# The low part of a mixing weight made by ScalarE and an adding transfer, with other changes around the RMS norms

## The chip, the cores and the metric

The kernel runs on one core of one Trainium2 chip. The metric is the device time of one execution in microseconds (us). TensorE is called PE here, VectorE DVE, ScalarE ACT, GpSimd POOL, and SyncE SP; SP's queue starts nearly all transfers of the kernel before. "PEld" is the loading of a product's stationary operand, which runs beside the products.

## What is computed

One layer of a hybrid decoder, in float32, for a prompt of 1024 tokens and 64 sample tokens (8 sequences of 8). The reference, cut to what matters:

```python
x = x + 0.5 * swiglu(rmsnorm(x, g1), ffn1_w_in, ffn1_w_out)      # D_FF = 2816
proj = rmsnorm(x, gm) @ w_in                                     # 1024 x 8224: u, z, x/B/C, dt, gates
branch_pool = pool_mix(u) @ pool_w_out                           # windowed means, 4 groups
y = ssd_scan(conv(x/B/C), dt)                                    # Mamba-2, chunks of 128
yg = y * silu(z);  yg = yg * rsqrt(mean(yg * yg per group of 512) + eps)
branch_ssd = (yg * ssd_norm) @ ssd_w_out
x = x + (sigmoid(g0) * branch_pool + sigmoid(g1) * branch_ssd) @ w_o
x = x + 0.5 * swiglu(rmsnorm(x, g2), ffn2_w_in, ffn2_w_out)
y = rmsnorm(x, norm_final)
```

## The kernel before, in words

**Tiling and stages.** Activations lie feature-major: 128 features on the partitions, tokens along the row. The tokens are worked in two halves: half 0 has 512 prompt tokens, half 1 has the other 512 and the 64 sample tokens (576). There are three stages, each with its own pool of buffers that is opened when the pool of the stage before is closed: `ffn1`, `mix` and `ffn2`. The mixing stage goes through half 0 and then half 1 (`mix_half`). In a half, PE first computes dt, then the pooling branch with its gate (tiles u, G0, `pool_w_out`), then four SSD groups. For each group it projects six conv tiles (`proj_group`), runs the scan as a chain beside the next group's projections, then z, then `ssd_w_out` of the group before; last come the gates, the merge and `w_o`.

**Precision.** A float32 matrix product is made of three products in a faster 32-bit format (float32r): weight and activation are each split into a rounded part hi and a rest lo, and PE adds hi·hi, hi·lo and lo·hi (`products`). A chunk of weights is 128 x 512 numbers (four blocks of 128 rows, 256 KB). `load_w` loads the chunk into a buffer `wraw` (6 buffers), ACT copies it rounded into `wh` (L274, 3 buffers), and DVE subtracts that from the chunk and writes the rest into `wl` (L275, 3 buffers). A chunk feeds 12 products of 512 columns in half 0, and 24 of 288 in half 1. The mixing stage uses 396 chunks. The SwiGLU stages use `load_w` too, for their first three column tiles (`ffn_in_plain`) and for the outgoing product; their other chunks go through `wino_weights`, which the change leaves alone.

**The RMS norms.** `rstd` is called 12 times: once for each half ahead of the mixing stage and once for each half ahead of ffn2 (by `norm_split` and `norm_parts`), and eight times in the gating of the SSD groups (`gating`). It squares and adds the tiles on ACT and DVE, sums over the partitions with one-column products on PE (`pss`, L160), and has the mean of 128 tokens in each column of a small tile `rsm`. `newton` then computes 1/sqrt on DVE: 11 small instructions (L322 to L327). After that PE transposes `rsm` (`prt`), ACT copies it out of PSUM (`rt`, L362), a transfer writes it to DRAM (`rd`, L363), and another reads it back, repeated on all 128 partitions, into `r` (L365). The tiles are multiplied by `r` on DVE (L1264 in the gating) and split again into hi and lo (L312 on ACT, L314 or L316 on DVE). `newton` is also used at the start, on the input blocks (`load_x`, L652 to L659), and at the end, in the final norm (L1431 to L1440).

**The order of the work.** The program is written as one stream of products; small chains (norms, scan, gating) are generators that are stepped between the products by a clock that counts the PE time written so far. A `yield 3.0` means "go on 3 us of PE time later". `R_WAIT0` is the wait between the reciprocal root and its transposition, and `R_WAIT` the wait between the transfer that reads `r` and its first use. Each engine works its own list in order. The weight split is written under `high_priority(40)`, which puts it earlier in the lists of ACT and DVE than where it is written.

Of the kernel before, what the change touches and what calls it, by code (L numbers as in the profile page):

```python
# [8 lines left out]
F32 = mybir.dt.float32  # L9
F32R = mybir.dt.float32r  # L10
I32 = mybir.dt.int32
AF = mybir.ActivationFunctionType
ALU = mybir.AluOpType

P = 128
# [20 lines left out]
N_ACT, N_BIG, N_PD = 58, 3, 4  # L36
N_RAW, N_W = 6, 3
N_FX, N_S, N_PDF = 17, 4, 6
# [11 lines left out]
MP = 2.0  # L50
R_WAIT0 = 3.0
R_WAIT = 5.0
F_Y = 0.5
# [8 lines left out]
def tile_hybrid_pool_ssd_macaron(  # L62
# [19 lines left out]
    def nm(s):  # L82
        uid[0] += 1
        return f"{s}_{uid[0]}"
# [78 lines left out]
    def tr(out, in_, idn):  # L163
        T.transpose(out, in_, idn)  # L164
        pe[0] += 0.107
# [10 lines left out]
    G.memset(ones, 1.0)  # L176


    rows = []
# [40 lines left out]
    Dcol = cp.tile([P, 16], F32, tag="Dcol", name="Dcol")  # L220
    rd_n = [0]
    hp = [0]
# [33 lines left out]

    ahead = {}

# [4 lines left out]
    def load_w(w, k0, nk, c0, ncol=P, behind=None):  # L263

        if (k0, c0) in ahead:
            return ahead.pop((k0, c0))
        raw, wh, wl = (sp.tile([P, 4 * P], d, tag=t, bufs=n, name=nm(t))[:, : nk * ncol]
                       for t, d, n in (("wraw", F32, N_RAW), ("wh", F32R, N_W), ("wl", F32R, N_W)))
        if behind is not None:
            hold(raw, behind)  # L270
        dma(raw.rearrange("p (k c) -> p k c", c=ncol),
            w[k0 * P : (k0 + nk) * P, c0 : c0 + ncol].rearrange("(k p) c -> p k c", p=P))
        with tc.high_priority(hp[0]):
            S.activation(wh, raw, AF.Copy)  # L274
            V.tensor_tensor(wl, raw, wh.bitcast(F32), op=ALU.subtract)  # L275
        return wh.rearrange("p (k c) -> p k c", c=ncol), wl.rearrange("p (k c) -> p k c", c=ncol)
# [40 lines left out]

    def newton(ss, fr):


        r, t = fr
        V.tensor_scalar(r.bitcast(I32), ss.bitcast(I32), -0.5, 1597463007.0, op0=ALU.mult, op1=ALU.add)  # L322
        V.tensor_scalar_mul(ss, ss, -0.5)
        for _ in range(3):
            V.tensor_tensor(t, r, r, op=ALU.mult)
            V.tensor_tensor(t, t, ss, op=ALU.mult)
            V.scalar_tensor_tensor(r, t, 1.5, r, op0=ALU.add, op1=ALU.mult)  # L327

    def rstd(tiles, h, count, out, pace=1.0):
# [23 lines left out]
        if h == 1:  # L353
            V.tensor_scalar(sm[:NS, 2, 4:5], pt[:NS, 4:5], 1.0 / count, EPS, op0=ALU.mult, op1=ALU.add)
        newton(v, (sm[:, 0, :nch], sm[:, 1, :nch]))
        yield R_WAIT0
        rd = dp.tile([5, P], F32, tag=f"rd{rd_n[0] % 4}", name=nm("rd"))
        rd_n[0] += 1
        pt = psum("ps", "prt")
        tr(pt[:nch, :P], sm[:, 0, :nch], ident)  # L360
        rt = act((P, P), name="rt")
        S.copy(rt[:nch], pt[:nch, :P])  # L362
        dma(rd[:nch], rt[:nch])  # L363
        r = act((P, N), name="r")
        dma(r, rd.rearrange("c p -> (c p)")[:N].partition_broadcast(P))  # L365
        yield R_WAIT
# [259 lines left out]
    def load_x(h, out):  # L626
# [26 lines left out]
        V.tensor_scalar(v, v, 1.0 / D, EPS, op0=ALU.mult, op1=ALU.add)  # L653
        newton(v, (ss[:, 2, :nb], ss[:, 3, :nb]))
        yield 0.5
# [766 lines left out]
    def final(g):  # L1422
# [9 lines left out]
        V.tensor_scalar(ss[:, 0, :nb], ss[:, 0, :nb], 1.0 / D, EPS, op0=ALU.mult, op1=ALU.add)  # L1432
        newton(ss[:, 0, :nb], (ss[:, 2, :nb], ss[:, 3, :nb]))
        for i, (_, dst, c0, n) in enumerate(parts[g]):
# [74 lines left out]
```

## Time and profile before

| | |
|---|---|
| time, median of 3 runs | 2989.13 us (2988.89 to 2989.58) |
| profiled execution: time, and span of its instructions | 2992.09 us, 2990.3 us |
| PE busy, share of the span | 2911.7 us, 97% |
| PEld | 2688.9 us, 90% |
| DVE | 1745.6 us, 58% |
| ACT | 1268.3 us, 42% |
| POOL | 410.3 us, 14% |
| mean granted TensorE clock | 0.993 |

How to read it: all times in the views count from the first instruction of the profiled execution. Its own time is 1.8 us above its span, and 3.0 us above the median of the runs. In a view of groups, a row has the line, the engine, the operation, what is written and read, the number of instructions, then the busy time, the mean ns of one, and the engine's idle time just before them with what ended it. In a timeline a row has start, length, engine, line and operation, the number of instructions merged into it, and in brackets the idle time before it with its releaser. A busy PE row is a modelled length, since products overlap; what counts for its pace is the distance from start to start.

### The profile page before, as it was taken

How to read it: one execution, taken by the hardware profiler on the slowest of the kernel's cores; microseconds unless marked ns; L12 is line 12 of the kernel's file. 1: busy time of each engine (PE TensorE's matmuls, PEld its weight loads, DVE VectorE, ACT ScalarE, POOL GpSimd, SP SyncE). 2: the span in 40 equal slices, each digit the busy share in tenths (PEclk: the TensorE clock that was granted, in tenths of full speed). 3: DMA queues.
4: the chain of work that ended last, by engine and by line, in shares of the span. 5: the costliest groups of instructions: out<-in, count | busy, mean ns of one | idle time of the engine just before them, and what ended most of it. 6: DMA issues, size and time to landing. Idle time of an engine off the chain costs nothing. (4 is left out here: it accounts for less than half of the span.)

```text
span 2990.3 us, 51513 instructions
## 1 busy us (share of the span) xinstructions
PE 2911.7 (97%) x19668; PEld 2688.9 (90%) x19668; DVE 1745.6 (58%) x3460; ACT 1268.3 (42%) x2560; POOL 410.3 (14%) x501
## 2 busy tenths in 40 slices
PE   7999999999999999999999999999999999999998
PEld 6999999789988878877999989999989999997898
DVE  6544344445373897877725987978775343444442
ACT  5343334433243665434424655543443333343432
POOL 5333333000000000000000110100023333330000
PEclk9999999999999999999999999999999999999999
DMA  4443223654334433445333344254443222235552
GB/s 137 137 130 100 70 83 98 220 171 121 105 100 121 115 103 96 117 119 172 101 101 107 97 127 137 84 141 134 152 136 97 77 84 69 84 95 170 173 160 71
DMA packets 519275, 352.09 MB, mean 118 GB/s; under 512 B 27163, under 2 KB 460433, under 8 KB 519019
## 3 DMA queue, kind: packets, MB, share of 16 engines
q1 hardware_dynamic: 519010, 348.80, 38.9%
q8 instruction: 154, 2.52, 0.3%
q14 instruction: 95, 0.77, 0.1%
q10 hardware_dynamic: 16, 0.00, 0.0%
HBM read 291.65 MB, written 57.29 MB: 117 GB/s over the span
## 5 line engine op out<-in xcount | busy, mean ns | idle before, releaser
L274 ACT ACTIVATE wh<-wraw 128x512 fp32r<-128x512 f32 (+1 forms) x636 | 391.5, 618 | 811.5 <-PE po L160 250.8
L275 DVE TENSOR_TENSOR wl<-wraw,wh 128x512 fp32r<-128x512 f32 (+1 forms) x636 | 438.0, 690 | 480.1 <-ACT wh L274 458.3
L160 PE MATMUL pw<-hi,wh 128*128 128x288 f32 (+1 forms) x1216 | 352.3, 290 | 4.0 <-DVE t L526 2.2
L160 PE MATMUL pw<-hi,wl 128*128 128x288 f32 (+1 forms) x1216 | 351.5, 289 | 0.0
L160 PE MATMUL pw<-lo,wh 128*128 128x288 f32 (+1 forms) x1216 | 351.2, 289 | 0.0
L160 PE MATMUL pw<-X,wh 128*128 128x288 f32 (+1 forms) x1824 | 347.4, 289 | 0.1
L160 PE MATMUL po<-hh,wh 128*128 128x288 f32 (+1 forms) x1056 | 289.4, 330 | 7.5 <-ACT hh L312 6.3
L160 PE MATMUL po<-hr,wh 128*128 128x288 f32 (+1 forms) x1056 | 289.4, 329 | 0.5 <-DVE hr L314 0.5
L160 PE MATMUL po<-hh,wl 128*128 128x288 f32 (+1 forms) x1056 | 289.0, 328 | 0.0
L160 PEld LDWEIGHTS pw<-X,wh 128*128 128x128 f32 x1824 | 288.1, 190 | 0.4 <-ACT t L522 0.4
L160 PE MATMUL pw<-X,wl 128*128 128x288 f32 (+1 forms) x912 | 263.0, 288 | 0.0
L160 PEld LDWEIGHTS pw<-hi,wh 128*128 128x128 f32 x1216 | 230.8, 190 | 4.9 <-DVE t L526 2.6
L160 PEld LDWEIGHTS pw<-lo,wh 128*128 128x128 f32 x1216 | 230.8, 190 | 0.0
L160 PEld LDWEIGHTS pw<-hi,wl 128*128 128x128 f32 x1216 | 230.8, 190 | 0.0
L422 DVE TENSOR_TENSOR wl<-s,wh 128x512 fp32r<-128x512 f32 x160 | 114.1, 714 | 175.6 <-ACT wh L421 172.8
L160 PEld LDWEIGHTS po<-hh,wh 128*128 128x128 f32 x1056 | 179.2, 189 | 26.5 <-ACT hh L312 11.4
L160 PEld LDWEIGHTS po<-hr,wh 128*128 128x128 f32 x1056 | 179.9, 189 | 17.8 <-DVE hr L314 4.1
L160 PEld LDWEIGHTS po<-hh,wl 128*128 128x128 f32 x1056 | 180.0, 189 | 14.4 <-DVE wl L275 0.9
L421 ACT ACTIVATE wh<-s 128x512 fp32r<-128x512 f32 x160 | 101.0, 632 | 179.8 <-PE pw L160 178.7
L160 PEld LDWEIGHTS pw<-X,wl 128*128 128x128 f32 x912 | 173.6, 190 | 0.0
L160 PE MATMUL pc<-hi,wh 128*128 128x288 f32 (+1 forms) x576 | 161.7, 333 | 0.0
L160 PE MATMUL pc<-hi,wl 128*128 128x288 f32 (+1 forms) x576 | 158.2, 328 | 0.0
(347 smaller groups left out, 6370.2 us busy)
## 6 DMA issues: line engine op xcount, KB each, us to landing
wraw<-in_w_in_dram SPq DMA_DIRECT2D x260, 256.0 KB
wraw<-in_ffn_w_in_dram SPq DMA_DIRECT2D x208, 256.0 KB
wraw<-in_ffn_w_out_dram SPq DMA_DIRECT2D x160, 256.0 KB
ab<-acsd SPq DMA_DIRECT2D x64, 256.0 KB
wraw<-in_ssd_w_out_dram SPq DMA_DIRECT2D x64, 256.0 KB
hd<-g SPq DMA_DIRECT2D x44, 288.0 KB
hr<-hd SPq DMA_DIRECT2D x44, 288.0 KB
hd<-g SPq DMA_DIRECT2D x44, 256.0 KB
```

Source lines behind the costliest of these rows:

```text
L160: T.matmul(out, lhsT, rhs, start=start, stop=stop, skip_group_check=free)
L274: S.activation(wh, raw, AF.Copy)
L275: V.tensor_tensor(wl, raw, wh.bitcast(F32), op=ALU.subtract)
L421: S.activation(wh, a, AF.Copy)
L422: V.tensor_tensor(wl, a, wh.bitcast(F32), op=ALU.subtract)
```

## The change

It has three parts.

1. In the mixing stage only, `load_w` no longer uses DVE. ACT makes a second, negated rounded copy of the chunk into a new buffer `wacc` (4 buffers, taken from the stage's own pool), and a transfer on POOL's queue reads the raw chunk and adds it to `wacc` in place (`accum_op`), so that `wacc` holds raw minus rounded. The rounded copy `wh` goes into the buffers named `wh` and `wl` by turns, so it has six.
2. The 11 DVE instructions of `newton` are replaced everywhere by one POOL instruction that raises to the power -0.5 (`rsqrt`).
3. In `rstd` the transposition and the way over DRAM are gone. PE multiplies a column of `rsm`, repeated 128 times as the stationary operand, with the identity (`along`, into a bank `prb`); that gives the 128 values along the row on all partitions. Four such products, and a fifth of 64 columns in half 1, are copied by ACT into `r`. `R_WAIT0` goes from 3.0 to 2.0 and `R_WAIT` from 5.0 to 0.5.

```diff
-N_RAW, N_W = 6, 3
+N_RAW, N_W, N_ACC = 6, 3, 4
-R_WAIT0 = 3.0
-R_WAIT = 5.0
+R_WAIT0 = 2.0
+R_WAIT = 0.5
+    mhalf = cp.tile([P, 8], F32, tag="mhalf", name="mhalf")
+    G.memset(mhalf, -0.5)
...
-        raw, wh, wl = (sp.tile([P, 4 * P], d, tag=t, bufs=n, name=nm(t))[:, : nk * ncol]
-                       for t, d, n in (("wraw", F32, N_RAW), ("wh", F32R, N_W), ("wl", F32R, N_W)))
+        mix = stage["name"] == "mix"
+        nth[0] += 1
+        raw, wh, wl = ((stage["p"] if t == "wacc" else sp).tile([P, 4 * P], d, tag=t, bufs=n, name=nm(t))[:, : nk * ncol]
+                       for t, d, n in (("wraw", F32, N_RAW), ("wl" if mix and nth[0] % 2 else "wh", F32R, N_W),
+                                       ("wacc" if mix else "wl", F32R, N_ACC if mix else N_W)))
...
             S.activation(wh, raw, AF.Copy)
-            V.tensor_tensor(wl, raw, wh.bitcast(F32), op=ALU.subtract)
+            if mix:
+                S.activation(wl, raw, AF.Copy, scale=-1.0)
+                G.dma_start(wl, raw, accum_op=ALU.add)
+            else:
+                V.tensor_tensor(wl, raw, wh.bitcast(F32), op=ALU.subtract)
...
-    def newton(ss, fr):
...
+    def rsqrt(r, ss):
+        G.tensor_tensor(r, ss, mhalf[: ss.shape[0], : ss.shape[1]], op=ALU.pow)
+    def along(out, r, i, n=P):
+        mm(out, r[:n, i : i + 1].broadcast_to([n, P]), ident[:n, :n])
...
-        newton(v, (sm[:, 0, :nch], sm[:, 1, :nch]))
+        rsqrt(sm[:, 0, :nch], v)
         yield R_WAIT0
-        rd = dp.tile([5, P], F32, tag=f"rd{rd_n[0] % 4}", name=nm("rd"))
-        rd_n[0] += 1
-        pt = psum("ps", "prt")
-        tr(pt[:nch, :P], sm[:, 0, :nch], ident)
-        rt = act((P, P), name="rt")
-        S.copy(rt[:nch], pt[:nch, :P])
-        dma(rd[:nch], rt[:nch])
         r = act((P, N), name="r")
-        dma(r, rd.rearrange("c p -> (c p)")[:N].partition_broadcast(P))
+        pr = psum("ps", "prb")
+        for c in range(4):
+            along(pr[:, c * P : (c + 1) * P], sm[:, 0], c)
+        S.copy(r[:, :512], pr)
+        if h == 1:
+            along(pt[:, 64:128], sm[:, 0], 4, NS)
+            S.copy(r[:, 512:], pt[:, 64:128])
         yield R_WAIT
```

The two other users of `newton` (`load_x`, `final`) call `rsqrt` in the same way.

In the rows that follow, a number behind a name is a buffer's number, which differs between the two programs. ACT's list at the beginning of the mixing stage, before: the last chunk of ffn1 (256 wide), then the mixing stage's chunks, and the first evacuation (`dfm`).

```order
L274 ACTIVATE wh_8755<-wraw_8754 128x256
L274 ACTIVATE wh_8796<-wraw_8795 128x512
L274 ACTIVATE wh_8814<-wraw_8813 128x512
L274 ACTIVATE wh_8835<-wraw_8834 128x512
L274 ACTIVATE wh_8853<-wraw_8852 128x512
L274 ACTIVATE wh_8886<-wraw_8885 128x512
L781 ACTIVATE dfm_8831<-pdt_8794,dtb 32x512
```

The same place now:

```order
L279 ACTIVATE wh_8726<-wraw_8725 128x256
L279 ACTIVATE wh_8786<-wraw_8785 128x512
L279 ACTIVATE wl_8767<-wraw_8766 128x512
L279 ACTIVATE wh_8827<-wraw_8826 128x512
L279 ACTIVATE wl_8808<-wraw_8807 128x512
L279 ACTIVATE wh_8880<-wraw_8879 128x512
L279 ACTIVATE wl_8861<-wraw_8860 128x512
L281 ACTIVATE wacc_8768<-wraw_8766 128x512
L281 ACTIVATE wacc_8787<-wraw_8785 128x512
L281 ACTIVATE wacc_8809<-wraw_8807 128x512
L281 ACTIVATE wacc_8828<-wraw_8826 128x512
```

The rounded copies of six chunks stand ahead of the first negated copy, `wacc_8768`, which belongs to the first chunk of all (`wraw_8766`). That instruction waits for the last transfer that writes x to DRAM at the end of ffn1 (L725), since `wacc` lies where a buffer of the closed stage lay.

PE's list at the first gating of half 0 (conv tiles `pc`), before:

```order
L160 MATMUL pc_11175<-hi_7962,wh_11236 128x512
L160 MATMUL pc_11175<-lo_7963,wh_11236 128x512
L160 MATMUL pc_11175<-hi_7962,wl_11237 128x512
L164 MATMUL prt_11222<-ident,rsm_11141 4x128
L160 MATMUL pc_11175<-hi_7992,wh_11236 128x512
```

And now, from the sums over the partitions (`pss`) on:

```order
L160 MATMUL pss_11197<-ones,ssq_11131 128x1 x4
L160 MATMUL pc_11167<-hi_7903,wh_11188 128x512
L160 MATMUL pc_11167<-lo_7904,wh_11188 128x512
L160 MATMUL pc_11167<-hi_7903,wacc_11189 128x512
L160 MATMUL pc_11167<-hi_7927,wh_11188 128x512
L160 MATMUL pc_11167<-lo_7928,wh_11188 128x512
L160 MATMUL pc_11167<-hi_7927,wacc_11189 128x512
L160 MATMUL pc_11167<-hi_7957,wh_11188 128x512
L160 MATMUL pc_11167<-lo_7958,wh_11188 128x512
L160 MATMUL pc_11167<-hi_7957,wacc_11189 128x512
L160 MATMUL prb_11215<-ident,rsm_11202 128x128 x4
```

One transposition has become four products; they stand nine products behind the sums.

POOL's list at the same place now (before, there are only the two rows of each conv tile here, a memset and a copy, L966 and L972):

```order
L282 DMA wacc_11293<-wraw_11291 128x512
L282 DMA wacc_11335<-wraw_11333 128x512
L329 TENSOR_TENSOR rsm_11202<-rsm_11202,mhalf 128x4
L282 DMA wacc_11359<-wraw_11357 128x512
L971 MEMSET craw_11254 128x3
L977 COPY chist<-craw_11254 128x3
L282 DMA wacc_11399<-wraw_11397 128x512
```

The power stands behind adding transfers in POOL's list, and those wait for ACT's negated copies.

More of the change, by code (lines that the diff above doesn't have):

```diff
@@ L220, in tile_hybrid_pool_ssd_macaron @@
     Dcol = cp.tile([P, 16], F32, tag="Dcol", name="Dcol")
-    rd_n = [0]
     hp = [0]
@@ L254, in tile_hybrid_pool_ssd_macaron @@
     dtd_sd = dp.tile([NS, NH], F32, tag="dtdsd", name="dtdsd")
-    ahead = {}
+    ahead, nth = {}, [0]
     def hold(t, src):
@@ L316, in split @@
             V.scalar_tensor_tensor(lo, src, scale, hi.bitcast(F32), op0=ALU.mult, op1=ALU.subtract)
-    def newton(ss, fr):
[L321 to L327, printed above, removed]
+    def rsqrt(r, ss):
+        G.tensor_tensor(r, ss, mhalf[: ss.shape[0], : ss.shape[1]], op=ALU.pow)
+    def along(out, r, i, n=P):
+        mm(out, r[:n, i : i + 1].broadcast_to([n, P]), ident[:n, :n])
     def rstd(tiles, h, count, out, pace=1.0):
@@ L653, in load_x @@
         V.tensor_scalar(v, v, 1.0 / D, EPS, op0=ALU.mult, op1=ALU.add)
-        newton(v, (ss[:, 2, :nb], ss[:, 3, :nb]))
+        rsqrt(ss[:, 2, :nb], v)
         yield 0.5
@@ L1432, in final @@
         V.tensor_scalar(ss[:, 0, :nb], ss[:, 0, :nb], 1.0 / D, EPS, op0=ALU.mult, op1=ALU.add)
-        newton(ss[:, 0, :nb], (ss[:, 2, :nb], ss[:, 3, :nb]))
+        rsqrt(ss[:, 2, :nb], ss[:, 0, :nb])
         for i, (_, dst, c0, n) in enumerate(parts[g]):
```

## The prediction

> **What bounds the kernel now.** I read three views, in this order. The page's busy times and the stage windows first: they say which engine sets the pace and in which stage it idles. The windows are the first input block, ffn1, the mixing stage, ffn2 and the tail; each figure is busy time, the count behind it in brackets.
>
> ```profile
> span 2990.3 us, 51513 instructions
> PE 2911.7 (97%) x19668; PEld 2688.9 (90%) x19668; DVE 1745.6 (58%) x3460; ACT 1268.3 (42%) x2560; POOL 410.3 (14%) x501
> ...
> 0.00:16.50 16.50, 0.24 (x1) 0.17 (x1) 4.50 (x19) 8.66 (x20) 2.37 (x20) 1.00 0.88 269
> 16.50:804.00 787.50, 773.06 (x5436) 737.11 (x5437) 363.02 (x653) 305.04 (x634) 182.57 (x177) 0.99 0.40 122
> 804.00:2213.00 1409.00, 1385.66 (x8941) 1233.89 (x8941) 1036.38 (x2190) 665.26 (x1321) 69.74 (x169) 1.00 0.41 119
> 2213.00:2973.50 760.50, 750.15 (x5272) 715.77 (x5273) 333.33 (x575) 283.77 (x571) 155.64 (x135) 1.00 0.35 107
> 2973.50:2990.30 16.80, 2.61 (x22) 2.00 (x19) 8.33 (x26) 5.54 (x14) 0.00 (x0) 0.70 0.40 141
> ```
>
> PE is busy everywhere but at the two ends. In the mixing stage, the only one where the weight split changes, it idles 1409 - 1385.7 = 23.3 us: nothing that takes load off DVE there can bring more than that, though DVE is busy for 1036 of the 1409 us. So I read second what PE waits for in that window (total us, times, longest), and third the same just behind it (from 2213 to 2300 us).
>
> ```profile
> PE pwo L160 <- DVE x L1366: 3.3, 2, 2.1
> PE pso L160 <- ACT yh L312: 3.0, 1, 3.0
> PE pso L160 <- DVE acc L1298: 2.8, 3, 1.5
> PE pso L160 <- DVE yl L316: 2.7, 4, 2.0
> PE prt L164 <- DVE rsm L327: 1.5, 4, 0.9
> PE pso L160 <- ACT craw L769: 1.3, 2, 1.0
> ```
>
> ```profile
> PE pu L160 <- DVE wl L275: 4.8, 3, 2.9
> ```
>
> These are single late hand-overs, in the main from DVE, and none of the first group is a weight split. Any product that is added to PE's list lengthens the kernel at once; any wait that goes is at most one of these.
>
> **The products for the norms: +9.7 us.** A norm loses one transposition and gets four float32 products of 128 columns. A float32 product stands in the trace as two instructions. Four products of this shape, and what follows them:
>
> ```profile
> 22.21 1.06 PE L160 MATMUL ptx<-dg,xin 128*128 128x128 f32 x8
> 23.02 0.48 PE L160 MATMUL pu<-hi,wh 128*128 128x512 f32 x1
> ```
>
> From start to start that is 0.81 us. Twelve norms make 12 x 0.81 = 9.7 us, and the fifth product of the six norms of half 1, half as wide, 6 x 0.1 = 0.6. The 12 transpositions that go I put at 0.05 us each, an estimate: they have a 128-column operand but one pass, a quarter of a product's 0.2. That gives 9.7 + 0.6 - 0.6 = 9.7 us. PE has no slack at ten of the twelve places, so I count it whole; with two of them in idle time it is 8, by the modelled 1.06 us it would be 12.7.
>
> **The stage's first chunk: +5.5 us.** Here is the change from ffn1 to mixing before: SP's write of the last x to DRAM, PE's first products of dt, and the third, which is the first to read a low part.
>
> ```profile
> 803.78 0.34 SPq L725 DMA_DIRECT2D xspill<-x  x1
> ...
> 803.90 0.47 PE L160 MATMUL pdt<-hi,wh 128*128 128x512 f32 x1 [0.88 <-DVE x L607]
> ...
> 804.21 0.39 PE L160 MATMUL pdt<-lo,wh 128*128 128x512 f32 x1
> ...
> 804.44 0.39 PE L160 MATMUL pdt<-hi,wl 128*128 128x512 f32 x1
> ```
>
> Before, `wl` came from a pool that is open in all stages, so the chunk was split ahead of time. Now `wacc` comes from the mixing stage's pool, its memory was a buffer of ffn1, and ACT's first negated copy waits for that write to land. Only then come the copy and the adding transfer, and PE, which works in order, stands at its third product. The nearest lengths of transfers, from the chain of waits (2 KB, and twice 256 to 288 KB), and of ACT's copy in the mixing window:
>
> ```profile
> 2004.80 4.08 DMA r<-rd
> 2110.82 2.08 DMA rd<-rt
> 2113.79 5.01 DMA ac<-accd
> ```
>
> ```profile
> L274 ACT ACTIVATE wh<-wraw 128x512 fp32r<-128x512 f32 x396 | 248.6, 629 | 496.3 <-PE pz L160 99.3 <-PE pg L160 76.6 <-PE pbp L160 69.1
> ```
>
> The write lands between 803.8 + 2.1 and 803.8 + 4.1; I take 806.3, since it comes when no other large transfer has just been started. With 0.63 for the copy it is 806.9, and with the adding transfer, for which the trace of before has no row, between 2.1 and 5.0 us, 3.0 taken as for a large one that runs nearly alone, it is 809.9. PE would have gone on at 804.4: a stall of 5.5 us, with ends of 4.2 and 9.0. The Trainium skill (DMA: Bandwidth & Descriptors, section on the anatomy of one DMA on the GpSimd path) fits such a transfer at 2.0 us plus its bytes over 436 GB/s, which would be an estimated 2.6 us for 256 KB and a stall of 5.1; no run here shows it yet.
>
> **Adding transfers in the steady state: nothing.** A `wacc` buffer comes free when PE has done a chunk, and is wanted again after three more. A chunk is 12 products, in the fence above 0.23 us apart (804.21 to 804.44), so there are 3 x 2.7 = 8.2 us in half 0; in half 1, 24 products of 288 columns take longer still. In that time must fit ACT's copy (0.63), the issue and the transfer (2.1 to 5.0): at most about 6.5 us. ACT has room for 396 x 0.63 = 249 us more in 1409 (665 + 249 = 914). What hides this is PE's own work; if the path grows past 8.2 us the cover is gone (a rival, below).
>
> **The power on POOL: start -1.9, tail -1.3, hand-overs +1.0 us.** At the start DVE did this, with PE waiting for `dg`:
>
> ```profile
> 12.26 0.17 DVE L653 TENSOR_SCALAR xss<-xss 128x4 f32<-128x4 f32 x1
> ...
> 13.78 0.69 DVE L275 TENSOR_TENSOR wl<-wraw,wh 128x512 fp32r<-128x512 f32 x1 [0.29 <-ACT wh L274]
> ...
> 16.16 0.87 DVE L659 TENSOR_SCALAR dg<-ident,xss 128x128 f32<-128x128 f32 x4
> ...
> 16.50 5.17 PE L160 MATMUL ptx<-dg,xin 128*128 128x128 f32 x24 [13.77 <-DVE dg L659]
> ```
>
> ```profile
> 2978.33 0.17 DVE L1432 TENSOR_SCALAR fss<-fss 128x5 f32<-128x5 f32 x1
> ...
> 2980.61 2.46 DVE L1440 TENSOR_SCALAR xtok<-xtok,fss 128x512 f32<-128x512 f32 x6
> ```
>
> The trace has no power on POOL. Its rows nearest to it are small copies and a larger two-operand instruction:
>
> ```profile
> L969 POOL COPY crs<-hist 128x24 f32<-128x24 f32 x24 | 19.9, 838 | 210.7 <-DVE hist L1009 156.8 <-DVE ct L983 50.3 <-DVE rsm L326 3.6
> L974 POOL COPY cst<-craw 128x3 f32<-128x3 f32 x24 | 9.7, 404 | 64.2 <-ACT craw L770 64.2
> L532 POOL TENSOR_TENSOR g<-g,t 128x256 f32<-128x256 f32 x38 | 28.4, 748 | 215.5 <-ACT g L529 215.5
> ```
>
> I take 0.6 us, nearest to the 3-column copy, and 0.1 for each hand-over: 0.8 in all, with ends of 0.5 and 2. At the start `dg`'s first part can then come at 13.2, but DVE's list has two splits between it and the other three parts. The later split ends at 14.47 whatever happens, so the four parts are done at 14.47 + 0.65 = 15.1 instead of 17.0: -1.9 us (0 if the power takes 2). In the tail the chain from 2978.50 to 2980.61 shrinks from 2.1 to 0.8: -1.3 us. In the norms the power has about nine products, 2.0 us, between the sums and its reader on PE, and can be held up by an adding transfer ahead of it on POOL, which itself waits for ACT; I allow 12 x 0.2 = 2.5 us of new waits for the 1.5 of `prt` above that go: +1.0, ends -1.5 and +10.
>
> **DVE's relief: -8 in the mixing stage, -1.5 behind it.** DVE loses 276 us there, and the norms lose about 5 us of latency over DRAM:
>
> ```profile
> L275 DVE TENSOR_TENSOR wl<-wraw,wh 128x512 fp32r<-128x512 f32 x397 | 276.1, 697 | 215.3 <-ACT wh L274 204.1 <-DMA wraw<-in_w_in_dram 10.0
> ```
>
> Of the waits quoted, 3.3 + 3.0 + 2.8 + 2.7 end with DVE or with an ACT step that DVE feeds; with the smaller ones, some 15 us of the 23.3. I take half, 8 us: `x` L1366 also waits for its load, and ACT, with a third more work, will be late at some of its own. Behind the stage DVE still does all of ffn2's splits, and only the shorter norm helps: 1.5 of 4.8 us.
>
> **The sum.** 9.7 + 5.5 - 1.9 - 1.3 + 1.0 - 8 - 1.5 = +3.5 us. On the profiled execution that is 2992.09 + 3.5 = 2995.6; its own 3.0 us above the median taken off, 2992.6, say 2993. A measurement of this kernel can tell about 0.2%, 6 us, from no change, so the likeliest result is one that hardly shows.
>
> **The rivals.** *Relief wins.* All the waits that DVE ends go (-15), and ffn2's 4.8; the stall at the stage costs its lower 4.2, the power is free (+0): 9.7 + 4.2 - 3.2 - 15 - 4.8 = -9, about 2980. For it: DVE's 74% in the stage before falls to 52%. Against: half of that must come from waits that have a second cause.
>
> *Adding transfers set the pace.* If copy, issue and transfer take 10 us instead of under 8.2, four buffers carry a chunk each (10 + 2.7) / 4 = 3.2 us instead of 2.7: 0.45 us on each of half 0's 198 chunks, half of them in dense runs, +45 us, about 3038. It decides from 8.2 us on. DVE can hold POOL up, as two splits of equal size show, the first of them beside work on POOL, the second not:
>
> ```profile
> 2196.26 1.23 DVE L275 TENSOR_TENSOR wl<-wraw,wh 128x512 fp32r<-128x512 f32 x1
> ...
> 2207.49 0.69 DVE L275 TENSOR_TENSOR wl<-wraw,wh 128x512 fp32r<-128x512 f32 x1
> ```
>
> The Trainium skill (SBUF — State Buffer, "Who interferes with whom") says why this may strike here: GpSimd writes the descriptors of its transfers through a port pair that some DVE instructions lock. The rows agree that the two engines get in each other's way, there at DVE's cost. Against this rival: a lock lasts one DVE instruction, under 1 us in all rows quoted, and the path has 1.7 us to spare.
>
> *ACT takes DVE's place.* ACT's 249 us more make it late as often as DVE was, and the relief is worth 1 us: 3.5 + 7 = +10.5, about 3000. For it: ACT already ends the waits for `yh` and `craw`. Against: at 65% it is less loaded than DVE was.
>
> *The small chains were nothing.* PE's idle time takes up the new products where they fall at waits, and the rest balances: within 3 us of 2989.
>
> **Chances.** The forecast 0.40, of which 0.25 lies within 0.2% and 0.15 above; relief wins 0.28, of which 0.24 shows; transfers set the pace 0.12; ACT in DVE's place 0.13; nothing 0.07. So faster 0.24, within 0.2% 0.36 (0.25, 0.04 and 0.07), slower 0.40. The range leaves out the slow transfers and a little of the best case: 2978 to 3012. The lower end is the relief's 2980 with two norms' products in idle time (8 for 9.7); the upper is the sum with 9.0 for the stall, 8 for the hand-overs, and 1 for the relief in all: 2989.1 + 9.7 + 9.0 + 8 - 3.2 - 1 = 3011.6.
>
> **What would show it.** Right: PE waits 4 to 9 us for `wacc` at the first dt product and nowhere else for more than 1 us; the four `prb` products take 0.8 us from start to start; PE's wait list loses the DVE rows by about half; `dg` comes near 14.5 us and the tail is 1.3 us shorter. Wrong: waits on `wacc` all through the dense runs (the second rival), powers of 2 us or more, or PE's idle time in the stage as large as before without the first stall.

## The result, and the profile after

The changed kernel takes 3032.05 us (median of 4 runs, 3030.54 to 3035.16), the kernel before in the same series 2989.36 us (2988.89 to 2991.04). The ratio is 1.0144, with a 95% interval of 1.0132 to 1.0157: 43 us slower, where I had forecast 4. The profiled execution took 3035.16 us, its span 3033.4 us. From here on, when a number behind a kernel's name is in brackets, it is its ratio to the kernel before, measured on the same chip, with the 95% interval.

First the page of the changed kernel: its span and busy times, the DMA engines' busy share in 40 slices, its DMA queues (packets, MB, share of the 16 engines' span), the two groups that the change adds, and the issues (KB each, median us from issue to landing).

```profile
span 3033.4 us, 52412 instructions
...
PE 2937.5 (97%) x19764; PEld 2702.5 (89%) x19764; DVE 1492.0 (49%) x2888; ACT 1472.2 (49%) x2962; POOL 761.0 (25%) x914
...
DMA  4443223753599888789888767787873222225552
...
q1 hardware_dynamic: 517174, 345.43, 38.2%
q0 software_dynamic: 57024, 103.83, 21.0%
...
L282 POOL DMA_DIRECT2D wacc<-wraw x396 | 343.0, 883 | 1039.5 <-ACT wacc L281 865.7
...
L281 ACT ACTIVATE wacc<-wraw 128x512 fp32r<-128x512 f32 x396 | 244.0, 620 | 7.6 <-PE pwo L160 2.6
...
wacc<-wraw POOLq DMA_DIRECT2D x396, 256.0 KB, 4.2
```

The DMA slices of the kernel before:

```profile
DMA  4443223654334433445333344254443222235552
```

The slices of the mixing stage (the eleventh to the thirtieth, roughly) went mostly from threes and fours to sevens and eights. The adding transfers are queue q0: 104 MB of the 453, but 21% of the engines' time, where the 345 MB of q1 take 38%. Per byte they hold the engines nearly twice as long as the rest (0.20% for a MB, against 0.11).

Second the window (PE, PEld, DVE, ACT and POOL busy, granted clock, DMA share, GB/s), here the mixing stage:

```profile
804.00:2255.00 1451.00, 1410.78 (x9028) 1249.61 (x9027) 789.67 (x1685) 867.08 (x1721) 404.80 (x573) 0.99 0.84 186
```

This window reaches 2 us into ffn2. From PE's first product of dt to its first product of ffn2 the stage takes 1449.7 us (803.15 to 2252.89) for 1409.2 (803.90 to 2213.12), so 40.5 of the 43 us lie there. PE's busy time took 24 of them and its idle time 17. DVE was relieved as meant, from 1036 to 790 us. The DMA share rose from 0.41 to 0.84. What PE waits for there:

```profile
PE pss L160 <- DVE ssq L346: 9.6, 3, 4.7
PE pdt L160 <- DMA wacc<-wraw: 7.4, 2, 5.1
PE ph0T L164 <- DMA h<-in_state_ssm_dram: 6.6, 7, 1.5
PE pwo L160 <- DMA wacc<-wraw: 2.2, 1, 2.2
PE pz L160 <- DMA wacc<-wraw: 2.1, 1, 2.1
```

The rows for `yh` and `yl` of before are gone. In their place stand loads: the state `h`, the reloaded x behind `ssq`, and four waits for `wacc`, 11.7 us in all, the first of them the stall that I had forecast.

A late load looks like this. At the end of half 0, eight tiles of x are read back (`xr`, 288 KB each) and squared on ACT; PE needs their sum. Before, from SP's first issue to ACT's last square:

```profile
1375.41 4.16 SPq L760 DMA_DIRECT2D xr<-xspill  x8
...
1382.85 1.82 ACT L339 ACTIVATE sq<-xr 128x576 f32<-128x576 f32 x3
1385.09 2.39 ACT L339 ACTIVATE sq<-xr 128x576 f32<-128x576 f32 x4
```

And after:

```profile
1394.77 5.84 SPq L765 DMA_DIRECT2D xr<-xspill  x8
1399.95 0.67 ACT L342 ACTIVATE ssq<-xr 128x576 f32<-128x576 f32 x1
...
1402.81 0.68 ACT L345 ACTIVATE sq<-xr 128x576 f32<-128x576 f32 x1 [1.62 <-DMA xr<-xspill]
1405.81 0.69 ACT L345 ACTIVATE sq<-xr 128x576 f32<-128x576 f32 x1 [2.31 <-DMA xr<-xspill]
1407.54 0.68 ACT L345 ACTIVATE sq<-xr 128x576 f32<-128x576 f32 x1 [1.05 <-DMA xr<-xspill]
1408.80 2.27 ACT L345 ACTIVATE sq<-xr 128x576 f32<-128x576 f32 x3 [0.57 <-DMA xr<-xspill]
...
1415.30 0.91 PE L160 MATMUL pss<-ones,ssq 128*128 128x1 f32 x7 [3.93 <-DVE ssq L346]
```

Before, ACT squares without a pause once the first tiles are there, and is done 12.1 us after the first issue. After, it waits between the tiles for the next one to land, is done after 16.3 us, and PE stands for 3.9 us.

### The profile page after: what moved, and what is told of

Same layout as the page of the kernel before. It is cut to its first block, busy times and chain, and to the rows that moved or that the text cites. A ratio compares the mean times of both kernels' runs of the same rounds, so it can differ in the third digit from the quotient of the medians.

```text
span 3033.4 us, 52412 instructions
## 1 busy us (share of the span) xinstructions
PE 2937.5 (97%) x19764; PEld 2702.5 (89%) x19764; DVE 1492.0 (49%) x2888; ACT 1472.2 (49%) x2962; POOL 761.0 (25%) x914
## 3 DMA queue, kind: packets, MB, share of 16 engines
q0 software_dynamic: 57024, 103.83, 21.0%
## 5 line engine op out<-in xcount | busy, mean ns | idle before, releaser
L282 POOL DMA_DIRECT2D wacc<-wraw x396 | 343.0, 883 | 1039.5 <-ACT wacc L281 865.7
L279 ACT ACTIVATE wh<-wraw 128x512 fp32r<-128x512 f32 (+1 forms) x438 | 267.1, 613 | 485.7 <-PE po L160 250.0
L284 DVE TENSOR_TENSOR wl<-wraw,wh 128x512 fp32r<-128x512 f32 x240 | 163.4, 683 | 250.3 <-ACT wh L279 237.6
L281 ACT ACTIVATE wacc<-wraw 128x512 fp32r<-128x512 f32 x396 | 244.0, 620 | 7.6 <-PE pwo L160 2.6
L279 ACT ACTIVATE wl<-wraw 128x512 fp32r<-128x512 f32 x198 | 124.1, 627 | 164.6 <-issue 48.4
```

Source lines behind the costliest of these rows:

```text
L281: S.activation(wl, raw, AF.Copy, scale=-1.0)
L282: G.dma_start(wl, raw, accum_op=ALU.add)
```

## The experiments

My theory after these traces, A: the adding transfers fill the DMA engines, so loads land late. The rivals: B, the path through four `wacc` buffers sets the pace; C, the norms cost the time; D, ACT's second copy does. F (POOL's work of starting the transfers) and G (the place of the buffers) came up on the way.

### The change in two halves: e1_norms_only, e2_lo_only, e16_power_only

The first is the changed kernel with `load_w` as before, the second the kernel before with the new `load_w`.

```diff
 e1_norms_only, against the changed kernel
-        mix = stage["name"] == "mix"
+        mix = False
```

> The change without its first part: the norms are new (power on POOL, products along the row, short waits), DVE makes the low parts as before. Theory A (the adding transfers load the 16 DMA engines, whose share of the mixing stage rises from 0.41 to 0.84, so loads come late): the norm part costs only its products on PE, about +12 us, less some 5 us of shorter chains: 2994 to 3002 us, DMA share of the mixing stage near 0.41, PE idle there 20 to 25 us. Theory C (the norm part is what costs: products, power, a short wait ahead of the first use of r): most of the 43 us are here, 3020 to 3035 us. Theory B (four wacc buffers set the pace): as A.

> The change's first part alone: ACT's negated copy and the adding transfer in the mixing stage; newton, the transposition and the way over DRAM as before. A and B: 43 us less the norm part, 3015 to 3027 us, DMA share of the mixing stage 0.8 or more, and the way of r over DRAM takes longer than before (its read took 4.08 us). C: 2990 to 3000 us.

Norms only took 2984.64 us (0.9985, 0.9976 to 0.9994), faster than the kernel before and than all that was expected. The lo part alone took 3067.41 us (1.0261, 1.0246 to 1.0276): 78 us slower, and 35 us slower than the whole change. C falls. A and B fall short on the second too, which had 3015 to 3027: the old norms and the new low parts hurt each other. How they do is not shown. In that kernel DVE waits for `r` to come back from DRAM:

```profile
DVE y L1271 <- DMA r<-rd: 19.0, 6, 6.9
...
DVE xn L387 <- DMA r<-rd: 13.2, 1, 13.2
...
DVE xn L716 <- DMA r<-rd: 8.8, 1, 8.8
```

That is 41.0 us, against 13.1 in the kernel before, where the two of `xn` are 2.5 and 1.7 and that of `y`

```profile
DVE y L1264 <- DMA r<-rd: 8.9, 6, 2.7
```

But these are waits of DVE. Of PE's 74 us of idle time in that stage, only some 10 stand at operands that are made with `r` (`yh`, `yl` and `hi`; 5.7 us before), and 28 at loads (the states, and the reloaded x behind `ssq`).

Why norms only gains, against my sum, was tried with the power alone:

```diff
 e16_power_only, against the kernel before
-        newton(v, (sm[:, 0, :nch], sm[:, 1, :nch]))
+        rsqrt(sm[:, 0, :nch], v)
```

> The kernel before, with the power on POOL for newton everywhere; the transposition, the way over DRAM and the old waits stay. By my sum: start -1.9, tail -1.3 (the power took 1.1 to 1.3 us, not 0.6, so -0.6), nothing in the norms: 2985 to 2988 us. If norms only (2984.6) owes its gain to the power: the same there, 2983 to 2986 us, and PE's idle time in the mixing stage falls to 12 us; if it owes it to the way over DRAM that goes, PE idles 20 us or more in that stage here.

(`load_x` and `final` likewise.) It took 2987.51 us (0.9997, 0.9988 to 1.0006): no change that can be told. PE's idle time in its mixing stage stays where it was, 1409 - 1384.6 = 24 us, while in norms only it is 1399 - 1386.3 = 13 us. The windows of the two, the power alone first:

```profile
803.00:2212.00 1409.00, 1384.60 (x8941) 1232.16 (x8941) 1022.82 (x2080) 665.24 (x1321) 80.71 (x176) 0.99 0.42 119
```

```profile
804.00:2203.00 1399.00, 1386.29 (x9021) 1237.84 (x9021) 1024.08 (x2081) 669.35 (x1327) 82.53 (x176) 1.00 0.41 118
```

So in the traces it is the way over DRAM whose end pays, together with the shorter `R_WAIT0` and `R_WAIT`, which no run parts from it; the medians (2984.6 and 2987.5) lie too close to prove it alone.

### A transfer, or DVE, for the addition: e3_dve_adds, e4_every_second, e15_dve_idle

```diff
 e3_dve_adds
-                G.dma_start(wl, raw, accum_op=ALU.add)
+                V.tensor_tensor(wl, raw, wl.bitcast(F32), op=ALU.add)
 e15_dve_idle
                 G.dma_start(wl, raw, accum_op=ALU.add)
+                V.tensor_tensor(idle[0], raw, wh.bitcast(F32), op=ALU.subtract)
```

> The changed kernel with one thing other: DVE adds the raw chunk to the negated copy in place, no transfer does. Buffers (four wacc of the stage's own pool), ACT's two copies and the norms stay. A: the DMA share falls back to about 0.41, PE's idle time with it; the stall at the first chunk stays in part, since wacc still lies where a buffer of the closed stage lay: 2997 to 3007 us. D (ACT's second copy costs, with 867 us busy of 1451): stays at 3025 to 3035 us. B: as A, since the path from the chunk to wacc is shorter too.

> The changed kernel, but DVE adds for every second chunk: 198 adding transfers, not 396. A: DMA share of the mixing stage near 0.62, and between a third and a half of the cost that 396 transfers have over none (late loads come more than in proportion as the engines fill): 3006 to 3018 us. B: two neighbouring buffers are never both held by a transfer, so the path is no longer short of buffers: as without transfers, 2997 to 3005 us.

> The changed kernel, and DVE subtracts for each chunk again, into a buffer that nobody reads (16-bit, for want of room): DVE keeps its work of before while the transfers make the low parts. This prices the relief of DVE, which I put at -8 us in the stage. If the relief is worth something beside the transfers, the time rises from 3032 to 3040 us or more; adding transfers that nobody read, with DVE's splits kept, cost 59 us over norms only, where the change costs 47, so I take 3044. If it is worth nothing: 3030 to 3035 us.

With DVE adding: 3001.92 us (1.0037, 1.0023 to 1.0051), DMA share 0.40. So 30 us of the 43 come with the transfers, and D falls as the main cause. With every second chunk by transfer: 3019.29 us (1.0097, 1.0080 to 1.0113), DMA share 0.61; 198 transfers cost 17 us and the other 198 another 13. A forecast "a third to a half" with the cost bending upwards; it is a little over half, so no bend can be told. B's 2997 to 3005 is out.

The third puts DVE's work back beside the transfers (0.69 us each, as in the kernel before): 3045.95 us (1.0189, 1.0170 to 1.0207), 14 us more than the change. So DVE's relief is worth 14 us there, and the transfers by themselves cost 3045.95 - 3001.92 = 44 us; the 30 are what is left of that. The waits of PE say where: with these transfers it waits 24.6 us at loads (the state `h` 9.0, `spin` 3.5, and the reloaded x behind `ssq`), with DVE adding 1.7. At `wacc` it waits 8.0 us and 2.3. The rows for the reloaded x, with the transfers and then with DVE adding:

```profile
PE pss L160 <- DVE ssq L347: 12.1, 3, 5.9
```

```profile
PE pss L160 <- DVE ssq L346: 0.6, 1, 0.6
```

### Transfers that nobody waits for: e5_idle_plain, e6_idle_adding, e9_idle_small

All three are norms only, with one transfer on POOL's queue for each chunk, into a buffer that no instruction reads.

```diff
 e6_idle_adding
             V.tensor_tensor(wl, raw, wh.bitcast(F32), op=ALU.subtract)
+            if xtra:
+                G.dma_start(dump[nth[0] % 4][:, : nk * ncol], raw, accum_op=ALU.add)
 e5_idle_plain: without accum_op
 e9_idle_small: dump[...][:, :16], raw[:, :16]
```

> The norms-only kernel (DVE makes the low parts), with one thing added: for each chunk of the mixing stage a plain transfer on POOL's queue copies the raw chunk to a buffer that nobody reads (256 KB, 396 times). No instruction of PE waits for it. A: the packets of such a copy take some 84 to 100 ns where adding ones take 198, so the DMA share of the mixing stage is near 0.6, and the time rises by 3 to 10 us over norms only. B (only the wait for wacc matters): no rise, within 2 us of norms only.

> The same, but the transfer that nobody reads is an adding one. A: DMA share of the mixing stage 0.8 or more, and nearly the whole cost of the changed kernel beyond norms and first chunk comes back though PE waits for no such transfer: 15 to 30 us over norms only, with waits for late loads (state, reloaded x). B: within 2 us of norms only. If PE's products themselves get slower beside the transfers (512 columns from 227 to 231 ns from start to start), that shows here too.

> The norms-only kernel (2984.6 us) with 396 adding transfers that nobody reads, as in the run that rose to 3043.6, but each of 16 columns instead of 512: as many instructions on POOL and as many rows, a thirty-second of the bytes. Theory A (the load on the DMA engines costs): DMA share of the mixing stage near that of norms only (under 0.55) and 2985 to 2995 us. Rival F (POOL's work of starting a transfer, 0.86 us each, and what it does to the DVE and POOL instructions beside it): most of the 59 us stay, 3020 us or more.

| kernel | us | ratio (interval) | DMA share of the mixing stage | PE idle there, us |
|---|---|---|---|---|
| e1_norms_only | 2984.64 | 0.9985 (0.9976 to 0.9994) | 0.41 | 12.7 |
| e9_idle_small | 2998.27 | 1.0033 (1.0023 to 1.0043) | 0.48 | 20.2 |
| e5_idle_plain | 3002.72 | 1.0039 (1.0025 to 1.0053) | 0.60 | 19.8 |
| e6_idle_adding | 3043.61 | 1.0182 (1.0165 to 1.0199) | 0.83 | 49.6 |

The windows of the last one, and its queue row, with the same row of the plain and of the small transfers:

```profile
804.00:2259.00 1455.00, 1405.36 (x9019) 1248.81 (x9017) 1023.47 (x2077) 667.05 (x1326) 422.14 (x582) 0.99 0.83 185
```

```profile
q0 software_dynamic: 57024, 103.83, 20.6%
```

```profile
q0 software_dynamic: 31680, 103.83, 9.2%
```

```profile
q0 software_dynamic: 57024, 3.27, 3.3%
```

Transfers of which no result is used cost 59 us over norms only: B cannot say that, and A expected it, though with 15 to 30 us (DVE keeps its work here, which the change takes away). Starting as many transfers of few bytes costs 14 us; that is F's share, less than its 3020 asked for and more than A's 2985 to 2995 had room for. The other 45 us come with the bytes, and with their being added: the same bytes copied plainly hold the engines for 9.2% of the span and not 20.6, and cost 18 us with their starts (A had 3 to 10). A packet of 2 KB takes 195 ns on the mean when it is added, a packet of the plain copy, which has 4 KB, 171, and the 2 KB packets of the loads 98. Adding, then, takes over twice the engines' time per byte, and that is what the loads run into. The eight reloads of x show it. With the idle adding transfers ACT's last square ends 14.6 us after the first issue:

```profile
1392.91 5.23 SPq L771 DMA_DIRECT2D xr<-xspill  x8
...
1406.05 1.49 ACT L348 ACTIVATE sq<-xr 128x576 f32<-128x576 f32 x2 [0.61 <-DMA xr<-xspill]
```

With the small ones it is 12.0 us, as in the kernel before (12.1):

```profile
1373.98 4.06 SPq L771 DMA_DIRECT2D xr<-xspill  x8
...
1383.58 2.39 ACT L348 ACTIVATE sq<-xr 128x576 f32<-128x576 f32 x4
```

No raw chunk is among these eight loads. Of the 2.6 us between the two, SP's eight starts take 1.2 (5.23 and 4.06 us); the rest comes after the last start, while ACT waits for tiles to land.

The idle transfers also have a way of their own that the change hardly has. They stand in POOL's list, wait there for the load of their chunk, and POOL's other work waits behind them. The largest wait of PE with the idle adding transfers, 7.9 us at `dh`, begins with a late memset on POOL:

```profile
835.59 1.75 POOL L287 DMA_DIRECT2D dump<-wraw  x2 [1.38 <-DMA wraw<-in_w_in_dram]
836.80 0.66 POOL L887 MEMSET uraw<- 128x15 f32 x1
837.49 0.71 DVE L910 TENSOR_TENSOR us<-uraw 128x526 f32<-128x526 f32 x1 [6.00 <-POOL uraw L887]
```

PE also waits 5.1 us there for the power on POOL, 3.6 with the small transfers, and 0.2 in the changed kernel. So the 59 and the 14 us show that transfers cost though nobody reads their result, but they are no exact price for those of the change; the 44 us above are nearer to one.

One more thing these runs don't part: a transfer that takes longer also holds its raw chunk longer, and SP's loads stand behind it in order. SP waited 31.5 us for such a chunk with the idle adding transfers, and 13.3 with the small ones; that is less than the 45 us, but not nothing. In the changed kernel such a wait is by far the largest of SP's queue in the mixing stage,

```profile
SPq L276 <- DMA wacc<-wraw: 1050.6, 379, 7.6
```

and in the kernel before the chunks were held until DVE's split, for a fifth less in all:

```profile
SPq L271 <- DVE wl L275: 824.7, 327, 10.3
```

### How many buffers, and the first chunk: e8_three, e11_five, e7_first_four_dve

```diff
 e8_three
-N_RAW, N_W, N_ACC = 6, 3, 4
+N_RAW, N_W, N_ACC = 6, 3, 3
 e11_five
+N_ACT, N_BIG, N_PD = 57, 3, 4
+N_RAW, N_W, N_ACC = 6, 3, 5
 e7_first_four_dve
+        n_mix[0] += stage["name"] == "mix"
+        mix = n_mix[0] > 4 and stage["name"] == "mix"
```

> The changed kernel with three wacc buffers for four. B (the buffers' path sets the pace): a path that is too long for four buffers is much too long for three, since a chunk then has 2 x 2.7 = 5.4 us for copy, issue and transfer (0.6 + 0.9 + 4.2 = 5.7): 3060 us or more. A: the time goes up little, 3032 to 3045 us, as the transfers come as fast as ACT and PE release them and the load on the DMA engines stays the same.

> The changed kernel with five wacc buffers for four; the room is taken from the activations (57 buffers for 58). With three buffers the time rose by 90 us. B (the path through four buffers sets the pace): 3005 to 3022 us, and PE's waits for wacc go. A (load on the DMA engines): the waits for wacc are only some 13 us of the stage, first chunk included, so 3024 to 3034 us, and the late loads stay.

> The changed kernel, but the first four chunks of the mixing stage are split by DVE as before, into buffers of the pool that is always open; the adding transfers begin with the fifth chunk. The stall at the first product of dt that reads a low part (5.06 us) goes: 4 to 5 us less than the changed kernel, near 3027 us, if PE doesn't lose it again at the fifth chunk. Same for A and B.

Three buffers: 3122.11 us (1.0443, 1.0427 to 1.0459), 90 us more than four. Five: 3028.97 us (1.0138, 1.0113 to 1.0163), not to be told from four. A had only 3032 to 3045 for three, and B was right that three are too few: a chunk then has 5.5 us, and copy, start and transfer take 0.62 + 0.88 + 4.2 = 5.7. PE's waits show it:

```profile
PE pc L160 <- DMA wacc<-wraw: 15.7, 13, 2.9
PE pg L160 <- DMA wacc<-wraw: 14.6, 16, 2.8
PE pwo L160 <- DMA wacc<-wraw: 12.0, 8, 3.9
```

With four there are 8.2 us, and more buffers bring nothing. B holds for three buffers and not for the change. Splitting the first four chunks on DVE gave 3029.77 us (1.0129, 1.0114 to 1.0144), 2.3 us less than the change; the interval takes in both no gain and the 4 to 5 us expected. PE then waits 2.6 us at the fifth chunk, the first that still needs `wacc`.

### Where the low parts lie: e10_dve_subtracts, e13_shift, e14_wh_three, e17_wh_three_pad, e18_after_pad

DVE's addition over ACT's negated copy was still 17 us slower than norms only. Here DVE subtracts again, but into `wacc`.

```diff
 e10_dve_subtracts
-                S.activation(wl, raw, AF.Copy, scale=-1.0)
-                G.dma_start(wl, raw, accum_op=ALU.add)
+                V.tensor_tensor(wl, raw, wh.bitcast(F32), op=ALU.subtract)
 e14_wh_three, besides
-("wl" if mix and nth[0] % 2 else "wh", F32R, N_W)
+("wh", F32R, N_W)
 e13_shift, against norms only
+        G.memset(stage["p"].tile([P, 4 * P], F32, tag="wacc", bufs=4, name=f"shift{i}"), 0.0)
 e17_wh_three_pad and e18_after_pad: e14_wh_three and the changed kernel, with
+    G.memset(stage["p"].tile([P, 16], F32, tag="pad", bufs=1, name="pad"), 0.0)
```

> The changed kernel's buffers and order (wacc in the stage's own pool, rounded copies in six buffers), but no negated copy and no transfer: DVE subtracts the rounded copy from the chunk, as before. Against the kernel in which ACT makes the negated copy and DVE adds (3001.9 us) only ACT's 396 copies go. D (ACT's 249 us more make it late): 2983 to 2990 us, near norms only (2984.6). G (the place of the buffers and the order cost the 17 us, not ACT): 2997 to 3005 us.

> The norms-only kernel with four buffers of the size of wacc in the mixing stage's pool that are zeroed once and then lie idle: everything behind them in that pool lies 8 KB further on, nothing else differs. With the change's buffers and DVE subtracting, PE's 512-column products came 231.0 ns apart for 227.4, without any wait, and the time was 12 us over norms only. If the activations' new place does that: 231 ns here too and 2992 to 2996 us. If it is where the weights lie: 227.4 ns and 2983 to 2987 us.

> The low parts in wacc, made by DVE's subtraction, as in the run at 2996.4 us; the rounded copies have only the three buffers named wh again, not six by turns. If the place of wacc slows PE's products: 231 ns and 2993 to 2999 us. If the six buffers by turns do: 227.4 ns and 2985 to 2990 us.

> The kernel with the low parts in wacc made by DVE's subtraction and three rounded buffers (2995.5 us, products of 512 columns 231.0 ns apart), with a tile of 64 bytes per partition ahead of wacc. wacc began 64 bytes past a multiple of 128 in each partition, wh and wl at a multiple of 128; now all do. If that start is what slows PE: 227.4 ns, some 8 us less, 2985 to 2990 us. If another thing of wacc's place does: 231 ns and 2993 to 2998 us.

> The changed kernel with the same 64 bytes ahead of wacc. If the start of the buffers slows PE: products of 512 columns 227.4 ns apart in place of 231.0, and 4 to 9 us less than the changed kernel, 3023 to 3028 us (less than 8 us if waits for late loads take up a part). If not: 3030 to 3035 us.

The first took 2996.39 us (1.0025, 1.0015 to 1.0034): between what D and what G had. 12 of the 17 us are G's, the buffers, and 5.5 are left for ACT's second copies, with an uncertainty of 5. Idle buffers in the same place cost nothing: 2985.02 us (0.9987, 0.9978 to 0.9997). With only three rounded buffers it stays at 2995.47 us (1.0024, 1.0014 to 1.0033). So it is `wacc` as an operand that slows the kernel, in dense stretches where PE waits for nothing. From 850 to 1000 us, norms only, then low parts in `wacc` with three rounded buffers:

```profile
850.00:1000.00 150.00, 150.00 (x667) 124.27 (x666) 78.80 (x125) 61.15 (x102) 2.73 (x17) 1.00 0.41 115
```

```profile
850.00:1000.00 150.00, 150.00 (x650) 121.90 (x649) 76.37 (x124) 60.05 (x100) 2.17 (x15) 1.00 0.40 112
```

In both, PE is busy for all of the 150 us at full granted clock, but it gets through 667 products in one and 650 in the other. The mean distance of 512-column products in half 0 is 227.4 ns in the kernel before, in norms only and in all three with idle transfers, and 231.0 in every kernel that reads low parts from `wacc`, with transfers or not. Over some 2260 such products that is 8 of the 12 us; products of 288 columns are not slower (132 to 133 ns in both kinds of kernel). The 64 bytes of padding did not mend it: 2999.05 us (1.0031, 1.0019 to 1.0043) and 231.2 ns, and on the changed kernel 3037.54 us (1.0149, 1.0132 to 1.0166). Only the pattern changed. Of the three products of a block (x's hi by `wh`, its lo by `wh`, its hi by `wacc`), the distances to the next were 228.4, 229.0 and 235.8 ns, and with the padding 226.7, 232.5 and 234.2; in norms only all are near 227. So the start of the buffers (64 bytes past a multiple of 128 by the program's layout, which no view shows) changes which products are slow, and is not why they are slow; what of the place does it stays open.

### POOL in DVE's place: e12_pool_subtracts

```diff
-                V.tensor_tensor(wl, raw, wh.bitcast(F32), op=ALU.subtract)
+                (G if turn else V).tensor_tensor(wl, raw, wh.bitcast(F32), op=ALU.subtract)
```

> The norms-only kernel, but POOL instead of DVE subtracts for every second chunk of the mixing stage: DVE is relieved of 138 us of its work there without a transfer. If DVE's load is what PE still waits for (my term for the relief, -8 us for the whole of it): 2978 to 2983 us. If the relief is worth nothing, or POOL's longer subtraction takes the place: 2984 to 2995 us.

It took 3037.13 us (1.0160, 1.0136 to 1.0184), 52 us over norms only and far above both ranges: relief of DVE, this time by POOL, and dearer than DVE's load. POOL takes 1401 ns for a subtraction, twice as long as DVE:

```profile
L285 POOL TENSOR_TENSOR wl<-wraw,wh 128x512 fp32r<-128x512 f32 x198 | 277.5, 1401 | 1004.1 <-ACT wh L280 807.1 <-DVE ab L1119 40.1 <-PE pz L160 36.6
```

DVE itself gets slower beside it. One of its frequent steps takes 860 ns here,

```profile
L989 DVE SCALAR_TENSOR_TENSOR ct<-craw,cwh,ct 128x512 f32<-128x512 f32 x144 | 123.9, 860 | 22.0 <-ACT ct L987 20.3
```

and 746 ns in norms only:

```profile
L988 DVE SCALAR_TENSOR_TENSOR ct<-craw,cwh,ct 128x512 f32<-128x512 f32 x144 | 107.4, 746 | 21.7 <-ACT ct L986 20.8
```

Which share of the 52 us is which was not tried further.

## Why the prediction was wrong, point by point

The runs can be chained, each with one thing more than the one ahead of it (medians): norms only -4.8 us against the kernel before; low parts in `wacc` and the other buffers +11.8 (e10 less e1); ACT's second copies +5.5 (e3 less e10); the adding transfers +44.0 (e15 less e3); DVE's subtraction gone -13.9 (the change less e15). They add up to the whole because each starts where the one ahead ends, so the sum proves nothing. Each step carries 4 to 7 us of uncertainty, and the +5.5 can hardly be told from nothing.

- **"Adding transfers in the steady state: nothing."** This is the step that failed: +44.0. What it compared was right. The path of a chunk takes 5.7 us of the 8.2 us that four buffers give, five buffers bring nothing, three are too few. But hiding its latency does not make a transfer free. I had 0.41 for the DMA share of that stage in a quoted row, and did not ask what 396 more transfers of 256 KB would make of it (0.84), nor who else waits on those engines. In the profiled executions of the two kernels of that step PE idles 18 and 52 us in the stage, and loses 7 and 20 us to a halved clock (last section): that is 34 and 14 more, near the 44. Idle adding transfers, whose result nobody reads, cost 59 us.
- **The transfer's length.** I took 3.0 us between 2.1 and 5.0; it is 4.2 from issue to landing, and 3.0 as a plain copy. The Trainium skill's fit (DMA: Bandwidth & Descriptors, anatomy of one DMA on the GpSimd path), an estimated 2.6 us, is under both, and the measurement decides.
- **The first chunk, +5.5.** Right: PE stands for 5.06 us at the product named, with the write, ACT's copy and the transfer in the order written. That the size is so near is in part luck: the write landed after 2.24 us (2.5 taken), the copy with its hand-over took 0.95 (0.63) and the transfer 3.6 (3.0), while PE did four more products ahead of the wait than I had counted.

```profile
803.04 0.34 SPq L730 DMA_DIRECT2D xspill<-x  x1
...
805.28 2.19 ACT L281 ACTIVATE wacc<-wraw 128x512 fp32r<-128x512 f32 x4 [2.08 <-DMA xspill<-x]
806.23 3.74 POOL L282 DMA_DIRECT2D wacc<-wraw  x4 [104.42 <-ACT wacc L281]
...
809.83 0.80 PE L160 MATMUL pdt<-hi,wacc 128*128 128x512 f32 x1 [5.06 <-DMA wacc<-wraw]
```

What I left out is the slow clock behind such a stall (last section), some 2 us more here. Taking the stall away moved the time by only 2.3 us, within the uncertainty, since part of it came back at the fifth chunk.
- **The products for the norms, +9.7.** The products are priced low: the 80 `prb` instructions of the stage hold PE for 10.4 us from start to start, 1.04 for a norm and not 0.81. But the norms as a whole gain 4.8 us. In norms only PE's idle time in the stage falls by 11 us and the time lost to a halved clock by 5, and about 5 more are saved in products that had been a little late each. That is relief that I had booked under DVE's splits. It comes with the way over DRAM that goes.
- **The power: -1.9, -1.3, +1.0.** It takes 1.28 us on the mean in the norms, and at the start and in the tail 1.03 and 1.17, not 0.6:

```profile
12.70 1.03 POOL L329 TENSOR_TENSOR xss<-xss,mhalf 128x4 f32<-128x4 f32 x1 [4.90 <-DVE xss L658]
```

`dg` is all done at 15.84 instead of 17.03 (-1.2), the mixing stage begins at 803.15 instead of 803.90 (which says little: in norms only it begins at 804.84, with three buffers at 800.83), the tail's chain takes 1.4 us instead of 2.1 (-0.7). Alone the power cannot be told from no change.
- **DVE's relief, -8 and -1.5.** In sign right and even too small in the stage: 14 us beside the transfers. Behind the stage there is none: from PE's first product of ffn2 to the end it is 780.5 us, and was 777.2.
- **Not in the sum at all:** the low parts' new place (+11.8, of which 8 are PE's slower products) and ACT's second copy (+5.5), which I had named only as a rival.
- **The rivals.** "Adding transfers set the pace" came out near the time, 3038, by another mechanism: four buffers are enough, and PE's waits for `wacc` are 11.7 us, 5.06 of them the forecast stall. My test for it (waits on `wacc` all through the dense runs) did not find it, and rightly. Two other signs of mine did point at the failure: PE waits for `wacc` three more times for over 2 us, and without the first stall it still idles 35 us in the stage, against 23. In the working against that rival one reading is wrong: not all DVE rows quoted are under 1 us, one is 1.23. "ACT takes DVE's place" had +7 and its size was near (+5.5). "Relief wins" falls.

## What to carry to other kernels

Moving work from an engine to the DMA queues moves it onto engines that every load of the stage shares: multiply the new bytes by what a packet of that kind costs, add it to the stage's DMA share, and ask which loads are issued only a few microseconds ahead of their use. That the latency of a transfer is hidden says nothing on that. And a change with two halves is best timed in halves: here one half was a gain of 5 us (0.9985, 0.9976 to 0.9994), faster than both kernels, and hidden under the other.

## What the runs showed of the hardware that I had not expected

**An adding transfer from SBUF to SBUF holds the DMA engines more than twice as long as a plain copy of the same bytes** (20.6% and 9.2% of a span of about 3000 us for 103.83 MB), and takes 4.3 us to land where the copy takes 3.0.

**A stall of PE can be paid twice.** After the 5.06 us at the first chunk the granted clock is 0.50 until 815.4 us, and the products come 0.43 us apart:

```profile
811.00:812.00 1.00, 1.00 (x4) 0.81 (x3) 0.00 (x0) 0.00 (x0) 0.00 (x0) 0.50 1.11 176
```

Eleven products of 512 columns pass at half speed, 11 x 0.2 = 2.2 us that the profile counts as busy PE. The Trainium skill (TensorE: Matmul & The Clock Gate, "What's actually happening") has PE fall to half rate after an idle window of some 3.4 us and stay there for about as long; the trace agrees on the rate and, with slow stretches of 3.4 or 6.8 us, on the length. But here a wait of 2.15 us (for `wacc`, at 1045.99 us) was enough: from 1048 to 1050 us the granted clock is 0.50 again. Not every such wait does it: one of 2.38 us, which ended at 1455.2, was not followed by a slow stretch. In the mixing stage the records of the granted clock show eight slow stretches in the changed kernel (41 us in all), three in the kernel before (14) and one in norms only (3.4). At half speed they cost half of that: 20, 7 and 2 us. Against norms only, PE's busy time in the stage grew by 23 us: 19 of slow clock and 8 for the place of `wacc`, with some 4 the other way.

**Products can be slower for where an operand lies**, without a wait and at full granted clock: 231.0 ns for 227.4. The cause is open.
